# First block's projections by seven block products, with every weight fold ahead of the values

## The chip, the core and the metric

The kernel runs on one core of one Trainium2 chip. TensorE multiplies, ScalarE and VectorE prepare its operands and take results out of PSUM, GpSimd (POOL) issues the transfers that add matrices up in DRAM, and SyncE (SP) issues nearly all other loads. The metric is the device time of one execution in microseconds, lower is better; the time of a kernel is the median of its runs.

## The reference

One decoder layer on a sequence of 2048 tokens of width 1024, and a final norm. This is the part around the change:

```python
h = rmsnorm(x, mix_norm_g[l])
proj = h @ w_in[l]
q, k, v, g, u = jnp.split(proj, [R, 2 * R, 3 * R, 4 * R], axis=-1)
y_ret = jax.nn.silu(g) * head_rmsnorm(retention(q, k, v, positions), ret_gn_g[l])
y_pool = pool_mixer(u, pool_w[l], pool_scale[l])
x = x + jnp.concatenate([y_ret, y_pool], axis=-1) @ w_out[l]
x = x + cross_attn(rmsnorm(x, xa_norm_g[l]), mem_n, xa_wq[l], xa_wkv[l], xa_wo[l])
x = x + conv_glu_ffn(rmsnorm(x, ffn_norm_g[l]), ...)
```

`retention` has four heads of 128 columns with rotary angles on queries and keys, and walks chunks of 128 tokens with a decayed state. `pool_mixer` takes trailing means over 2, 4, 8 and 16 tokens in four groups of 128 columns, subtracts the token and multiplies each group by a 128 x 128 matrix. The cross-attention looks at 256 memory tokens.

## The kernel before, in words

Everything is held transposed: 128 features on the partitions, tokens along the row. The sequence is cut into two blocks of 1024 tokens (`T`), each into two halves of 512 (`SUB`). Every f32 operand is split into a rounded high part and the remainder, by ScalarE and VectorE (`split`, L254), and every product of two such pairs is three matmuls (`passes`, L267; L269 to L271): high by high, high by low, low by high.

**Folds.** Weight matrices that are only ever used one after the other are multiplied ahead of the tokens (`folded_weights`, L423). The memory's keys and values are sixteen projections (`project`, L464), each with eight by three matmuls 256 columns wide. Then for each of four heads the query matrix is folded with the keys into score weights `Md` (L522), and the values with the output matrix into `VWd` (L542); for each of four pooling groups the group's matrix is folded with its rows of the output projection into `WPd` (L566). The results leave by stores that ScalarE issues (`keep`, L487). It is a generator: `folded(n)` (L1998) runs n of its 28 steps. The first sixteen steps, the memory's keys and values, come before block 0's values, with the loads of block 0's x between them (`load_x_wide`, L597; `squares_wide`, L603). The other twelve steps are spread over block 0's heads (`per`, L2033, and `folded(100)`).

**Block 0's projections.** `values` (L732) computes the value columns for all tokens. `head_inputs` (L750) computes gate, query and key columns of one head, each column tile by `unit` (L315): two halves times eight features' tiles times three matmuls, 48 of 512 columns. `pool_group` (L690) does the same for the four pool tiles. The rotary tables are made beside the values (`rope_tables`, L612), after the norm's factors, and scaled by them (`rope_scale`, L671).

**Block 1's projections.** `head_projections` (L1639) takes sixteen column tiles in eight pairs (`PAIRS`, L34) and computes each pair, for the two halves of the 1024 features and the two halves of the tokens, as a two by two block matrix product with seven block products in place of eight (the Winograd form of Strassen's scheme). Each block product is four by three matmuls of 512 columns. What it needs besides: sums of the blocks of x (`quarter_sums`, L1603, on ScalarE and VectorE beside the values), sums of the weights' blocks in DRAM (`Ad`), and additions of results as they leave PSUM (`Heads.evac`). The feed-forward part uses the same scheme for up and down.

**Weight sums.** `weight_sums` (L1012) makes `Ad`, `Ud` (up) and `Dd` (down) by DMAs from DRAM to DRAM that GpSimd issues, four plain and four accumulating ones of 256 KB for each of 8, 22 and 12 jobs. A job takes four turns. A turn comes every `spacing[0]` calls, and each turn waits on a small ScalarE instruction. Before, it starts after the last fold, with spacing 7.

**Order.** The program is written in the order in which steps are yielded, and a scheduling pass then orders each engine's queue; `keep_in_program_order` and `issue_after` pin some instructions. Buffers rotate: five raw buffers of 512 KB for weights (`raws`), three pairs for their split forms (`prs`), ten temporaries (`TT`), five PSUM banks for projections.

Of the kernel before, what the change touches and what calls it, by code (L numbers as in the profile page):

```python
# [136 lines left out]
def trunk(ctx, tc, xT, memT, pos, w_qkgu, w_v, wkv, wqT, wo, wout_r, wout_p, poolT, w_up, w_dn, vecs, consts, outT):  # L137
# [27 lines left out]
    Z = new_z(F32)  # L165
# [257 lines left out]
    def folded_weights():  # L423
# [4 lines left out]
        bank = []  # L428
        raws, first = [Z.take() for _ in range(2)], [new_raw()]
        for q in range(4):  # L430
            to = raws[q // 2].f[:, q % 2 * SUB : (q % 2 + 1) * SUB].rearrange("p (k m) -> p k m", m=NMEM)
            sp.dma_start(to, memT.rearrange("(k p) m -> p k m", p=P)[:, 2 * q : 2 * q + 2])
            if q < 2:
                sp.dma_start(first[0][:, q * SUB : (q + 1) * SUB], wkv[0][:, 4 * q : 4 * q + 4].rearrange("p k n -> p (k n)"))
        first.append(load_tile(wkv[1]))
# [5 lines left out]
        parts = []  # L441
        for k in range(KT):
            h, j = divmod(k, 4)
            split(raws[h].f[:, j * NMEM : (j + 1) * NMEM], mh[:, k], ml[:, k], memg[:, k : k + 1], kept="both")
            if k in (0, 3):
                parts.append(new_pair())
                split(first[0][:, k // 3 * SUB : (k // 3 + 1) * SUB], parts[-1][:, 0], parts[-1][:, 1], kept="both")
        first[0] = parts
        rm = TT.take()
        rn = smp.tile([P, 4], F32, tag="rnm", name="rnm", bufs=1)[:, :2]  # L450

        def memory_norm():
            for r in raws:
                tc.keep_in_program_order(act.activation(r.f, r.f, AF.Square))
            f, other = (r.f for r in raws)
# [4 lines left out]
            for r in raws:  # L460
                r.free()
            spread(rn, [rm.f[:, :NMEM]])

        def project(n):  # L464

            if n < 2:
                hs = first[0] if n == 0 else pairs(first[1])
            else:
                hs = pairs(load_tile(wkv[n]))
# [4 lines left out]
            for k in range(KT):  # L474
                w = [hs[k // 4][:, i, (k % 4) * P : (k % 4 + 1) * P] for i in range(2)]
                passes(ps, w, (mh[:, k], ml[:, k]), k == 0, k == KT - 1)
            return ps

        def row_pairs(src):
            raw = new_raw()  # L480
            sp.dma_start(raw, src)
            u = B.take(2)
            for i in range(2):
                split(raw[:, i * SUB : (i + 1) * SUB], u.r[:, i * SUB : (i + 1) * SUB], u.r[:, T + i * SUB : T + (i + 1) * SUB])
            return u
# [8 lines left out]
        kk = B.take(4)  # L494
        kp4 = kk.r.rearrange("p (n i m) -> p n i m", i=2, m=NMEM)
        ps = [project(n) for n in range(2)]
        sp.dma_start(cs_t, consts)
        memory_norm()
        for n in range(KT):
            if n > 1:  # L500
                ps.append(project(n))
            if n % 2:
                for at in (n - 1, n):
                    t = TT.take()
                    tt(dve, t.f[:, :NMEM], ps.pop(0), rm.f[:, :NMEM], ALU.mult)
                    split(t.f[:, :NMEM], kp4[:, at, 0], kp4[:, at, 1])
                    t.free()
            if n == KT - 1:
                rm.free()
            yield  # L510
        vv = B.take(4)
        vp4 = vv.r.rearrange("p (n i m) -> p n i m", i=2, m=NMEM)
        for n in range(KT):
            ps.append(project(KT + n))
            if n % 2:
                for at in (n - 1, n):
                    split(ps.pop(0), vp4[:, at, 0], vp4[:, at, 1])
            if n == KT - 1:
                mp.free()
            yield  # L520

        for h in range(HEADS):  # L522
            dp = [row_pairs(wqT[(2 * h + dt) * P : (2 * h + dt + 1) * P, :]) for dt in range(2)]
            for k2 in range(KT // 2):
                ps = mmps()
                for j in range(2):
                    for dt in range(2):
                        k = 2 * k2 + j
                        w = [dp[dt].r[:, i * T + k * P : i * T + (k + 1) * P] for i in range(2)]
                        passes(ps[:, j * NMEM : (j + 1) * NMEM], w, (kp4[:, 2 * h + dt, 0], kp4[:, 2 * h + dt, 1]), dt == 0, dt == 1)  # L530
# [5 lines left out]
            for u in dp:  # L536
                u.free()
            if h == HEADS - 1:
                kk.free()
            yield  # L540

        for h in range(HEADS):  # L542
            dp = [row_pairs(wo[(2 * h + dt) * P : (2 * h + dt + 1) * P, :]) for dt in range(2)]
            for mt in range(2):
                for nh in range(2):
                    ps = mmps()
                    for dt in range(2):
                        lh = [vp4[:, 2 * h + dt, i, mt * P : (mt + 1) * P] for i in range(2)]
                        w = [dp[dt].r[:, i * T + nh * SUB : i * T + (nh + 1) * SUB] for i in range(2)]
                        passes(ps, lh, w, dt == 0, dt == 1)  # L550
# [3 lines left out]
            for u in dp:  # L554
                u.free()
            if h == HEADS - 1:
                vv.free()
            yield

        raw = new_raw()  # L560
        r3 = raw[:, :SUB].rearrange("p (g c) -> p g c", g=4)
        sp.dma_start(r3, poolT.rearrange("g p c -> p g c"))
        pw = B.take()
        tt(dve, r3, r3, bcast(pscale, P), ALU.mult)
        split(raw[:, :SUB], pw.r[:, :SUB], pw.r[:, SUB:])
        for g in range(4):  # L566
            u = row_pairs(wout_p[g])
            for nh in range(2):
                ps = mmps()
                lh = [pw.r[:, i * SUB + g * P : i * SUB + (g + 1) * P] for i in range(2)]  # L570
                passes(ps, lh, [u.r[:, i * T + nh * SUB : i * T + (nh + 1) * SUB] for i in range(2)], True, True)
# [3 lines left out]
            u.free()  # L575
            if g == 3:
                pw.free()
            yield
# [18 lines left out]
    def load_x_wide(k, room):  # L597

        f = room[k].f
# [3 lines left out]
    def squares_wide(k, room):  # L603

        f = room[k].f
        tc.keep_in_program_order(act.activation(f, f, AF.Square))
        if k:
            tc.keep_in_program_order(tt(dve, room[0].f, room[0].f, f, ALU.add))
            room[k].free()

# [60 lines left out]
    def rope_scale(tabs, rb):  # L671

        cos, sin = tabs
        out = Z.take(2)
        for s in range(NS):
            ps = slice(64 * s, 64 * s + 64)
            r = rb[s].f[ps, :SUB]
            for hf in range(2):
                po = slice(64 * hf, 64 * hf + 64)
                tt(dve, out.f[po, s * SUB : (s + 1) * SUB], cos.f[ps, :SUB], r, ALU.mult)  # L680
                dve.scalar_tensor_tensor(
                    out=out.f[po, T + s * SUB : T + (s + 1) * SUB],
                    in0=sin.f[ps, :SUB], scalar=1.0 if hf else -1.0, in1=r, op0=ALU.mult, op1=ALU.mult,
                )
        cos.free()
        sin.free()
        return out


    def pool_group(b, g, rb):  # L690
        out = B.take(2)

        def evac(s, ps):
            u, *bufs = [TT.take() for _ in range(3 if g else 2)]
            tt(dve, u.f[:, 16 : 16 + SUB], ps, rb[s].f[:, :SUB], ALU.mult)
            dve.tensor_copy(u.f[:, 0:16], phalo[:, g])
            dve.tensor_copy(phalo[:, g], u.f[:, SUB : SUB + 16])
            src, lo = u, 1
            for i in range(g + 1):
                sh = 1 << i  # L700
                dst = bufs[i % 2]
                tt(dve, dst.f[:, lo : 16 + SUB], src.f[:, lo : 16 + SUB], src.f[:, lo - sh : 16 + SUB - sh], ALU.add)
                src = dst
                lo += 2 * sh
            cur, d = u.f[:, 16 : 16 + SUB], src.f[:, 16 : 16 + SUB]
            w = 2 << g
            if b == 0 and s == 0:
                tt(dve, d[:, :w], d[:, :w], icnt[:, :w], ALU.mult)
                ts(dve, d[:, w:], d[:, w:], 1.0 / w, ALU.mult)
                tt(dve, d, d, cur, ALU.subtract)  # L710
            else:
                stt(d, d, 1.0 / w, cur, ALU.mult, ALU.subtract)
            split(d, out.r[:, s * SUB : (s + 1) * SUB], out.r[:, T + s * SUB : T + (s + 1) * SUB])
            for r in (u, *bufs):
                r.free()

        unit(load_tile(w_qkgu[12 + g]), xpair, evac)
        return out


    def value_weights(kp, room=None):
        raw = new_raw() if room is None else room.f
        sp.dma_start(raw.rearrange("p (k n) -> p k n", k=2), w_v[2 * kp : 2 * kp + 2].rearrange("k p n -> p k n"))
        u = B.take(2)
# [3 lines left out]
        if room is not None:  # L728
            room.free()
        return u  # L730

    def values(rn, wp, step=lambda: None, v=None):  # L732
        v = v or Z.take(4)
# [16 lines left out]
    def head_inputs(h, rb, cs, fill):  # L750
# [1562 lines left out]
```

## Time and profile before

| | |
|---|---|
| median of 3 runs | 2430.71 us (2430.0 to 2430.91) |
| profiled execution, first to last instruction (the page gives it no other time) | 2429.8 us |
| instructions | 33360 |
| moved by DMA | 502.35 MB |

How to read it: an engine's busy time is the time in which it executed something; PE stands for TensorE's matmuls, PEld for its loading of weights, DVE for VectorE, ACT for ScalarE. A row of the table of stretches gives one stretch of the execution. A group of instructions gives its line, engine and operation, its output and inputs, shapes, count, then busy time, mean duration of one, and the engine's idle time just before them with what ended it. A row of the waits gives who waited for whom, the total, the number of times, and the longest. In a row of the timeline stand start and duration in us. A DMA queue's row gives packets, MB and the time of its packets as a share of 16 engines; q1 carries SyncE's transfers, q10 ScalarE's, q0 GpSimd's.

### The profile page before, as it was taken

Reading aid. Unit: us, or ns where it says so; the run is one execution under the profiler, and the core shown is the slowest. Engines: PE = TensorE matmul, PEld = TensorE weight load, DVE = VectorE, ACT = ScalarE, POOL = GpSimd, SP = SyncE. Lnnn points to the kernel's source line nnn. Section 1 sums busy time; section 2 is a strip of 40 time slices with the busy share of each in tenths; the row PEclk is TensorE's granted clock in tenths of the full one; section 3 lists DMA queues with packets and bytes.
Section 4 is the critical chain, followed back from the end, with each engine's and each line's share of the span. In section 5 each row is a group of like instructions: output and inputs, shape, how many; then the busy total and the mean of one; then the engine's idle time right before and its main releaser. Section 6 shows DMA issues by size and latency. Waiting matters only on the chain.

```text
span 2429.8 us, 33360 instructions
## 1 busy us (share of the span) xinstructions
PE 2412.5 (99%) x11328; PEld 2018.4 (83%) x11328; DVE 1722.6 (71%) x2911; ACT 1292.3 (53%) x2360; POOL 306.1 (13%) x477
## 2 busy tenths in 40 slices
PE   9999999999999999999999999999999999999998
PEld 8888888888888888888888888888888888888887
DVE  7756566655857775565788776887677698867875
ACT  6434423444545553334655555765555577666663
POOL 0000012154032444300001010020000000000000
PEclk9999999999999999999999999999999999999999
DMA  7233548699678899985568564755556479758951
GB/s 283 76 105 115 163 137 225 189 237 329 203 206 216 197 254 305 258 293 168 173 223 272 170 204 143 249 191 164 173 158 211 126 244 311 238 183 279 348 178 73
DMA packets 263627, 502.35 MB, mean 207 GB/s; under 512 B 28832, under 2 KB 58016, under 8 KB 263456
## 3 DMA queue, kind: packets, MB, share of 16 engines
q1 hardware_dynamic: 201424, 385.78, 48.3%
q0 software_dynamic: 37376, 86.00, 15.3%
q10 hardware_dynamic: 24656, 28.43, 3.4%
q8 instruction: 89, 1.46, 0.2%
q14 instruction: 82, 0.67, 0.1%
HBM read 398.65 MB, written 187.43 MB: 241 GB/s over the span
## 4 chain that ended last, share of the span: by engine, by line
PE 98%; DVE 1%; ACT 1%; DMA 0%; issue 0%; SPq 0%; DVEq 0%; ACTq 0%
PE mm L269 31%; PE mm L271 30%; PE mm L270 30%; PE aux L269 1%; PE aux L270 1%; PE aux L271 1%; PE aux L832 1%; PE aux L816 1%; PE aux L957 1%; PE aux L805 1%; PE aux L834 1%; DVE Z L241 0%; PE aux L350 0%; PE aux L807 0%; DMA R<-wkv 0%; PE aux L857 0%
## 5 line engine op out<-in xcount | busy, mean ns | idle before, releaser
L269 PE MATMUL mm<-G,Q 128*128 128x512 f32 (+1 forms) x1703 | 656.1, 386 | 3.8 <-ACT Q L257 2.5
L271 PE MATMUL mm<-G,Q 128*128 128x512 f32 (+1 forms) x1703 | 652.9, 384 | 1.4 <-DVE Q L241 1.4
L270 PE MATMUL mm<-G,Q 128*128 128x512 f32 (+1 forms) x1575 | 605.2, 384 | 0.4 <-DVE G L249 0.3
L270 PE MATMUL mm<-G,E 128*128 128x512 f32 x1084 | 421.5, 389 | 0.0
L269 PE MATMUL mm<-G,E 128*128 128x512 f32 x1084 | 420.0, 389 | 0.0
L271 PE MATMUL mm<-G,E 128*128 128x512 f32 x1084 | 419.3, 389 | 0.0
L269 PEld LDWEIGHTS mm<-G,Q 128*128 128x128 f32 x1703 | 320.1, 188 | 67.6 <-ACT Q L257 3.4
L271 PEld LDWEIGHTS mm<-G,Q 128*128 128x128 f32 x1703 | 320.1, 188 | 64.5 <-DVE Q L241 2.0
L270 PEld LDWEIGHTS mm<-G,Q 128*128 128x128 f32 x1575 | 296.0, 188 | 57.3 <-DVE G L249 0.8
L241 DVE TENSOR_TENSOR Z<-Z,mm 128x512 f32<-128x512 f32 (+1 forms) x310 | 207.6, 674 | 121.5 <-PE mm L271 115.7
L249 DVE SCALAR_TENSOR_TENSOR Z<-Z,vecs 128x1024 f32<-128x1024 f32 x176 | 224.8, 1281 | 50.2 <-ACT Z L1191 47.9
L271 PEld LDWEIGHTS mm<-G,E 128*128 128x128 f32 x1084 | 203.5, 188 | 42.4
L270 PEld LDWEIGHTS mm<-G,E 128*128 128x128 f32 x1084 | 203.6, 188 | 42.2
L269 PEld LDWEIGHTS mm<-G,E 128*128 128x128 f32 x1084 | 203.5, 188 | 42.1
L1128 ACT ACTIVATE E<-R 128x512 fp32r<-128x512 f32 (+1 forms) x165 | 101.4, 615 | 144.2 <-PE mm L270 138.3
L241 DVE TENSOR_TENSOR Q<-R,Q 128x512 fp32r<-128x512 f32 x158 | 108.1, 688 | 73.2 <-ACT Q L257 56.0
L241 DVE TENSOR_TENSOR T<-T 128x512 f32<-128x512 f32 (+3 forms) x202 | 138.6, 690 | 21.1 <-ACT T L416 12.1
L241 DVE TENSOR_TENSOR G<-T,G 128x512 fp32r<-128x512 f32 (+1 forms) x185 | 121.6, 677 | 26.5 <-ACT G L1075 13.5
L1075 ACT ACTIVATE G<-T 128x512 fp32r<-128x512 f32 x186 | 112.0, 623 | 32.4 <-DMA T<-Gd 25.7
L1191 ACT ACTIVATE Z<-Z,vecs 128x1024 f32<-128x1024 f32 x88 | 109.1, 1241 | 31.2 <-DVE Z L241 30.2
L1128 ACT ACTIVATE E<-S 128x512 fp32r<-128x512 f32 (+1 forms) x107 | 65.9, 616 | 108.6 <-PE mm L270 106.5
L241 DVE TENSOR_TENSOR E<-R,E 128x512 fp32r<-128x512 f32 (+1 forms) x129 | 86.6, 673 | 44.6 <-ACT E L1128 42.7
(356 smaller groups left out, 3838.2 us busy)
## 6 DMA issues: line engine op xcount, KB each, us to landing
T<-Gd SPq DMA_DIRECT2D x173, 256.0 KB, 4.5
Ud<-w_up POOLq DMA_DIRECT2D x132, 256.0 KB, 9.3
Gd<-Z SPq DMA_DIRECT2D x110, 256.0 KB, 2.8
R<-Ud SPq DMA_DIRECT2D x106, 256.0 KB, 2.7
R<-w_up SPq DMA_DIRECT2D x80, 256.0 KB, 3.1
S<-Ud SPq DMA_DIRECT2D x70, 256.0 KB, 2.8
Gd<-T SPq DMA_DIRECT2D x56, 256.0 KB, 3.4
S<-w_up SPq DMA_DIRECT2D x52, 256.0 KB, 3.2
```

The costliest lines, as they stand in the source:

```text
L241: return eng.tensor_tensor(out=out, in0=a, in1=b, op=op)
L249: return dve.scalar_tensor_tensor(out=out, in0=a, scalar=s, in1=b, op0=op0, op1=op1)
L269: pe.matmul(ps, lh, rh, start=start, stop=False, skip_group_check=more)
L270: pe.matmul(ps, lh, rl, start=False, stop=False, skip_group_check=more)
L271: latest[0] = pe.matmul(ps, ll, rh, start=False, stop=stop, skip_group_check=more)
L805: pe.matmul(col(sc, c), self.ch(k, c), self.ch(q, c), start=True, stop=True)
L816: pe.matmul(col(self.kv, c), col(self.kn.f, c), self.ch(v, c, h * T), start=True, stop=True)
L832: pe.matmul(col(y, c), col(self.pr.f, c), self.ch(v, c, h * T), start=True, stop=self.cur[c] is None)
L834: pe.matmul(col(y, c), self.ch(q, c), self.cur[c], start=False, stop=True)
L1075: one = act.activation(hi, x, AF.Copy, scale=-1.0 if i == 2 else 1.0)
L1128: act.activation(p2[:, 0, :w], self.raw[i].f[:, :w], AF.Copy)
L1191: act.activation(self.c[g].f, a[:, 2:], AF.Identity, bias=cb[:, f : f + 1], scale=cw[2][:, f : f + 1])
```

## The change

1. Block 0 takes the path of block 1 for its query, key, gate and pool columns: `quarter_sums`, `head_projections` and the first three output tiles with weights fetched ahead. `head_inputs`, `pool_group` and `rope_scale` are gone, and `retention` loses its second form.
2. All 28 steps of the folds, and one that frees buffers, run ahead of the values, in a written order in which the memory's projections alternate with the folds that use them. Weights of the folds are split 1024 columns at a time into five wide pairs (four of them in `Z`, one in `Q`) rather than 512 at a time. Keys and values leave PSUM two tiles at a time.
3. x is loaded beside the folds, its squares are added up as each tile arrives, in raw buffers; value weights follow later.
4. Block 0's rotary tables are made at the first keys and stored to DRAM, from where `head_projections` reads them.
5. The weight sums start in the folds' last steps with spacing 2; the eight jobs for these columns start every second turn.

```diff
+        K, V, M, O, W = keys, memory_values, score_weights, output_weights, pool_weights
+        for f, *a in ((K, 0), (K, 1), (K, 2), (K, 3), (K, 4), (K, 5), (M, 0), (K, 6), (K, 7), (M, 1), (V, 0), (V, 1), (M, 2),
+                      (V, 2), (V, 3), (M, 3), (V, 4), (V, 5), (O, 0), (V, 6), (V, 7), (O, 1), (W, 0), (W, 1), (O, 2),
+                      (W, 2), (W, 3), (O, 3), (none_left,)):
+            f(*a)
             yield
...
+        zr = new_z(F32R).t
+        wides = Places([(Q, 0)] + [(zr, 2 * i * T) for i in range(4)], 2 * T)
...
+        def wide_pair(raw, parts=1):
+            u, w = wide(), T // parts
+            for i in range(parts):
+                split(raw[:, i * w : (i + 1) * w], *(r[:, i * w : (i + 1) * w] for r in u))
+            return u
...
         while jobs or live:
-            if jobs:
+            if jobs and (len(jobs) <= others or at % 2 == 0):
                 live.append(jobs.pop(0))
...
+    under[0], spacing[0] = weight_sums(), 2
+    wv, total, tables0 = [], None, stored_tables(0)
+    for n, _ in enumerate(folded_weights()):
+        if n in (1, 2, 3, 4):
+            for _ in range(3):
+                next(tables0, None)
+        if n == 3:
+            total = raws.take()
+        if n in (4, 6, 8, 10, 12, 14, 16, 18):
+            load_x_wide((n - 4) // 2, total)
+        if n == 19:
+            normed = norm_tables([total], late=True)
+        if n in (18, 21):
+            wv.append(value_weights(len(wv), 0))
+        if n in (24, 25):
+            wv.append(value_weights(len(wv), 1))
+        if n > 19:
+            next(under[0], None)
+    Z = new_z(F32)
+    slow[0], paced[0] = False, True
     for b in range(NB):
-        if b == 0:
-            rn, rb, last = normed
-            v = values(lambda: rn, wv)
...
-            per = [(0, 1, 1), (0, 1, 1), (0, 2, 2), (0, 2, 3)]
-            mix = []
-            for h in range(HEADS):
-                qkg = head_inputs(h, rb, cs, lambda i: folded(per[h][i]))
-                mix.append(B.take(2))
-                behind[0] = retention(b, h, qkg, v, mix[h])
-            folded(100)
-            slow[0], paced[0], spacing[0] = False, True, 7
-            pooled = {g: pool_group(b, g, rb) for g in (0, 3, 2, 1)}
...
+        t1, t2 = (B.arenas[0].take(4) for _ in range(2))
+        v, z = Z.take(4), Z.take(4)
+        more_sums = quarter_sums(b, t1, t2, z)
+        next(more_sums)
+        got, place = [], [0]
+        heads = head_projections(b, v, normed[1], t1, t2, z, got)
+
+        def between():
+            next(behind[0], None)
+            if b == 0:
+                next(under[0], None)
```

More of the change, by code (lines that the diff above doesn't have):

```diff
@@ L459, in memory_norm @@
             dve.tensor_copy(rn, stats([f[:, :NMEM]]))
-            for r in raws:
+            for r in memory:
                 r.free()
-            spread(rn, [rm.f[:, :NMEM]])
+            spread(rn, [rm.f[:, :NMEM]], late=True)
         def project(n):
[L466 to L469, printed above, removed]
+            u = u0 if n == 0 else wide_pair(second, 2) if n == 1 else wide_pair(load_tile(wkv[n]))
             if n % 2 == 0:
@@ L690, in pool_group @@
[L690 to L718, printed above, removed]
@@ new lines, in trunk, with weight_half @@
+    Z = new_z(F32)
+    slow[0], paced[0] = False, True
+    for b in range(NB):
+        t1, t2 = (B.arenas[0].take(4) for _ in range(2))
[8 more added lines that the diff above has]
+                next(under[0], None)
+            place[0] += 1
+            for _ in range(2 if place[0] > 2 else 1):
+                next(more_sums, None)
+            if place[0] > 6:
+                if place[0] == 7:
+                    for _ in more_sums:
+                        pass
+                    next(heads)
+                next(heads)
+        values(lambda: normed[0], wv, between, v)
+        finish()
+        rb = normed[1]
+        got.append(v)
+        parts = [next(heads)]
+        mix = got[1]
+        def weight_half():
+            return parts.pop() if parts else next(heads)
```

410 lines of the change are left out of this document (131 added, 279 removed).

## The prediction

> **What bounds the kernel now.** I read the page's head and its chain of waits first, then the table of stretches, then who waits for whom on TensorE, then groups of instructions by shape.
>
> ```profile
> span 2429.8 us, 33360 instructions
> PE 2412.5 (99%) x11328; PEld 2018.4 (83%) x11328; DVE 1722.6 (71%) x2911; ACT 1292.3 (53%) x2360; POOL 306.1 (13%) x477
> PE 98%; DVE 1%; ACT 1%; DMA 0%; issue 0%; SPq 0%; DVEq 0%; ACTq 0%
> ```
>
> TensorE is the chain. A saved matmul is worth its whole step, if nothing else comes last in its place. So I need the step, the places where TensorE does wait, and the load of the other engines wherever the change packs work. In the stretches below, the columns are busy time and count of PE, PEld, DVE, ACT and POOL, then clock, DMA share and GB/s.
>
> ```profile
> 0.00:5.39 5.39, 4.09 (x18) 3.90 (x18) 1.27 (x8) 2.78 (x5) 0.20 (x4) 1.00 0.64 189
> 5.39:42.52 37.13, 35.20 (x272) 33.37 (x272) 32.00 (x67) 27.75 (x48) 0.00 (x0) 1.00 0.89 349
> 42.52:49.40 6.88, 4.74 (x26) 4.54 (x25) 6.88 (x12) 5.72 (x10) 0.00 (x0) 0.75 0.52 175
> 20.00:40.00 20.00, 20.00 (x169) 20.00 (x168) 17.76 (x41) 14.02 (x25) 0.00 (x0) 1.00 0.90 353
> 400.00:420.00 20.00, 20.00 (x90) 16.58 (x89) 9.26 (x15) 6.00 (x11) 1.38 (x3) 1.00 0.91 260
> ```
>
> A 512-wide matmul steps in 20/90 = 0.2222 us, a 256-wide one in 20/169 = 0.1183 us. TensorE loses time only at the start: 272 matmuls need 32.2 us of the second row's 37.13 (4.9 lost), 26 need 3.1 of the third's 6.88 (3.8 lost). In 20 to 40 us it is never idle although VectorE is 89% busy and DMA 90%: close to full, this pipeline still works.
>
> **Part by part. Removed: products.** Block 0's sixteen column tiles took 16 x 2 halves x 8 x 3 = 768 matmuls; eight pairs of seven products take 8 x 7 x 4 x 3 = 672. 96 fewer at 0.2222: **-21.3 us**. Retention and values keep their matmuls.
>
> **Moved: the folds.** Of the scores', output's and pool's folds, 192 matmuls of 256 columns and 120 of 512 leave the head stage, where they cost TensorE their steps and nothing else, and join the 384 of the memory's keys and values. TensorE's part is 576 x 0.1183 + 120 x 0.2222 = 94.8 us; after the 5.4 us before the first fold matmul and the 4.9 us lost early, folds would end at **105.1 us** if TensorE set it. The third row's 3.8 us lies in that stage too; it goes if the new stage is last elsewhere: **-3.8**. The question is what else the stage must do by then. ScalarE's rows:
>
> ```profile
> L606 ACT ACTIVATE Z<-Z 128x1024 f32<-128x1024 f32 x8 | 7.8, 1044 | 0.0
> L260 ACT ACTIVATE G<-Z,vecs 128x1024 fp32r<-128x1024 f32 x8 | 9.1, 1141 | 0.1
> L260 ACT ACTIVATE G<-Z,vecs 128x256 fp32r<-128x256 f32 x8 | 3.6, 499 | 2.1 <-DMA Z<-memT 2.1
> L454 ACT ACTIVATE Z<-Z 128x1024 f32<-128x1024 f32 x2 | 2.0, 1043 | 0.0
> L257 ACT ACTIVATE Q<-R 128x512 fp32r<-128x512 f32 x36 | 22.3, 629 | 48.6 <-PE mm L270 45.7 <-PE aux L374 1.4 <-DMA R<-wkv 0.8
> L534 ACT ACTIVATE T<-mm,vecs 128x256 f32<-128x256 f32 x32 | 13.3, 470 | 6.9 <-PE mm L271 5.2 <-PE aux L857 1.4 <-ACT G L257 0.3
> L552 ACT ACTIVATE T<-mm,rnm 128x512 f32<-128x512 f32 x16 | 11.0, 687 | 7.1 <-PE mm L271 6.9 <-DMA VWd<-T 0.2
> L665 ACT ACT_TABLE_LOAD x1 | 1.3, 1283 | 0.0
> ```
>
> Weights are now split 1024 wide: 16 + 8 + 8 + 4 = 36 splits. No plain one of that width is in the trace; it lies between 7.8/8 = 0.98 and 9.1/8 = 1.14, and I take 1.06: 38.0 us (35 to 41). x: 8 x (1.14 + 0.98) = 16.9. Memory: 3.6 + 2.0. Evacuations: 13.3 + 11.0, and the pool's eight at the 0.62 of L257, 5.0. Splits of 512 (keys, values, value weights, pool): 17 x 0.62 = 10.5. Sines, sign and factor copies with a table load: about 4.5. Sum 104.7 us. And ScalarE issues the 40 stores:
>
> ```profile
> 299.52 0.37 ACTq L488 DMA_DIRECT2D WPd<-T  x1
> 312.62 1.07 ACT L573 ACTIVATE T<-mm 128x512 f32<-128x512 f32 x2
> 313.23 0.93 ACTq L488 DMA_DIRECT2D WPd<-T  x2
> 314.26 1.09 ACT L573 ACTIVATE T<-mm 128x512 f32<-128x512 f32 x2 [0.57 <-ACT T L573]
> 314.88 1.99 ACTq L488 DMA_DIRECT2D WPd<-T  x2
> 317.48 0.60 ACT L573 ACTIVATE T<-mm 128x512 f32<-128x512 f32 x1 [2.14 <-DMA WPd<-T]
> ```
>
> An issue costs 0.37 us, or nothing where it lies beside the instruction before it: 0 to 14.8 us, half taken. In the rows two evacuations with two issues took 1.64 us (312.62 to 314.26) where two alone take 1.07, so half an issue each is shown. ScalarE's first split started at 4.1 us, hence 4.1 + 104.7 + 7.4 = **116 us** (109 to 124). VectorE:
>
> ```profile
> L241 DVE TENSOR_TENSOR Z<-Z 128x1024 f32<-128x1024 f32 x7 | 8.6, 1224 | 1.8 <-ACT Z L454 1.1 <-ACT Z L606 0.3
> L249 DVE SCALAR_TENSOR_TENSOR G<-Z,vecs,G 128x1024 fp32r<-128x1024 f32 x8 | 10.2, 1281 | 0.4 <-issue 0.4
> L249 DVE SCALAR_TENSOR_TENSOR T<-T 128x512 f32<-128x512 f32 x13 | 8.7, 689 | 0.2
> L241 DVE TENSOR_TENSOR T<-T 128x512 f32<-128x512 f32 x4 | 2.8, 692 | 0.1
> L246 DVE TENSOR_SCALAR T<-T 128x512 f32<-128x512 f32 x6 | 2.6, 426 | 0.1
> ```
>
> 36 low parts at 1.23 are 44.3; x 10.2 + 8.6; memory about 6; 21 of 512 at 0.69 (keys, values, value weights, pool) 14.5; the rotary tables, now at the first keys, 13 + 4 + 9 operations, 8.7 + 2.8 + 3.9 = 15.4; norms and factors 7.5. Sum 106.5, from 4.6 us: **111 us**. The tables and the split of x are queued ahead of later low parts on VectorE, and TensorE waits for those.
>
> DMA, in turn the first reads, the two kinds of stores, and the weight sums:
>
> ```profile
> DMA packets 3032, 10.60 MB, mean 408 GB/s; under 512 B 321, under 2 KB 321, under 8 KB 3029
> q10 hardware_dynamic: 4880, 4.46, 12.1%
> q10 hardware_dynamic: 6871, 3.41, 21.4%
> q0 software_dynamic: 2428, 5.35, 62.0%
> q1 hardware_dynamic: 2424, 4.41, 32.1%
> ```
>
> They come from 10 to 36, 130 to 240, 246 to 300 and (the last two) 700 to 740 us. Reads run at 408 GB/s; stores at 4.46 MB / (12.1% of 110 us) = 335 GB/s in long rows and 3.41 / (21.4% of 54) = 295 in short ones; sums at 5.35 / (62% of 40) = 216. The stage reads 27.3 MB (wkv 8.4; x, wq and wo 4.2 each; 6.3 of others): 66.9 us. It stores 10.5 MB of folds and 0.8 of tables: 36.2. Five turns of sums queued on POOL before the values are 19 transfers of 0.262 MB: 23.0. That is 126 us, of which some 17 may land after the last fold: the last stores, eight buffers in flight, the last turn. So **110 us**.
>
> Three resources end at 110 to 116 us where TensorE alone ends at 105.1. Each waits for another, so I add 4 us to the longest (the early 4.9 us of the second row is such a loss): 120, **+14.9** (+4 to +25).
>
> When dense matmuls resume, the clock can be low:
>
> ```profile
> 42.24 0.28 PE L270 MATMUL mm<-G 128*128 128x256 f32 x1
> 44.27 0.39 PE L269 MATMUL mm<-G,Q 128*128 128x256 f32 x1 [1.75 <-ACT Q L257]
> 46.07 0.42 PE L271 MATMUL mm<-G 128*128 128x256 f32 x1
> 46.28 0.41 PE L269 MATMUL mm<-G 128*128 128x256 f32 x1
> ```
>
> After 1.75 us of idleness the steps were 0.21 us instead of 0.12, in a stretch whose granted clock was 0.75: some sixteen steps, 1.5 us. Where TensorE isn't last that is hidden; I count one such spell, ahead of the values: **+1.5** (0 to 3). The Trainium skill, "TensorE: Matmul & The Clock Gate", section "Why this matters for your kernels", asks only for no gaps above about 3 us; by it this term would be nil and the sum 1.5 us lower. The shorter gap here was followed by the lower clock, so the row decides.
>
> **Moved: heads, sums, tables.** Block 0's heads now run as block 1's do, whose whole idleness is
>
> ```profile
> PE aux L805 <- DVE E L249: 1.1, 1, 1.1
> PE mm L269 <- ACT T L1752: 0.8, 1, 0.8
> ```
>
> **+1.9**. Their sums in DRAM must be ready: one job begins every second turn and takes four turns. Five turns come before the values and eight beside them, so the first five pairs' sums are complete when the heads begin and the others by about their tenth product, while a pair's seven products last 7 x 12 x 0.2222 = 18.7 us: none is late. Weights for up and down follow at one turn per two products, denser than in block 1. Mixing, attention and the rest keep their order; nothing counted.
>
> Sum: -21.3 - 3.8 + 14.9 + 1.5 + 1.9 = -6.8 us, span 2423.0. The page gives the profiled execution no time but its span, 0.9 us under the 2430.71 median of the runs: **2424.0 us**. About 0.2% (4.9 us) is what a measurement can tell from no change.
>
> **Rivals.** *Hidden (0.12):* issues cost nothing and values are drawn in among the folds, so that the stage loses 2 us or less beyond TensorE's time: -21.3 - 3.8 + 2 + 1.9 + 0 gives 2409.5; up to 2416. For it: the 20 to 40 us row. Against: four loads at once.
>
> *The last folds starve (0.22), slower:* from the first output fold to the last pool fold TensorE has 96 x 0.2222 + 48 x 0.1183 = 27 us. Its reads are 9.2 MB (22.5 us), its stores 5.25 (17.8), its sums 14 transfers (17.0): 57 us. Eight stores in flight (7.1) and four weight buffers ahead (5.1) leave 45, a stall of 18; with 7 us of ScalarE's and VectorE's before it, 25 in the place of 14.9: 2434.1; without the buffers 2446. The row at 317.48 speaks for it: ScalarE waited 2.14 us for a store there, and TensorE had other work then, which it now hasn't. It decides once the folds end after 105.1 + 21.7 = 126.8 us.
>
> *Sums starve the heads (0.08):* a job is 2.1 MB, 9.7 us at 216 GB/s, and one is due per 5.3 us, beside the products' 0.262 MB per 2.67 us. If those loads fall behind by 0.1 to 0.3 us in each of 56 products, 6 to 17 us are added: 2430 to 2441. Against: with q0 at 62% beside q1, loads were met and TensorE was full. "DMA: Bandwidth & Descriptors" of the Trainium skill, section "Queues, rings and completion order", has each engine take queues in turn by packets; by it the loads keep half, and the rows agree, both queues moving.
>
> *The change doesn't do it (0.02):* were the folds not all ahead, head matmuls would still alternate with them; the time would be near the hidden case.
>
> Likeliest, the sum above (0.50): 2416 to 2429.5; a third of it lies within 0.2%. The rest (0.06) is spread. Faster: 0.35 + 0.12 + 0.06 = 0.53; same 0.19; slower 0.28. The range leaves out the ends of hidden and starved: 2411 to 2439.
>
> **What would show it.** Right: 96 fewer wide products, the folds' last matmul near 120 us, ScalarE over 90% busy until then, TensorE waits there of 10 to 15 us on splits and evacuations. Wrong: TensorE full there (hidden), evacuations waiting for stores with folds past 127 us (starved), or waits on Ad or w_qkgu loads in block 0's heads.

## The result and the profile after

| | before | after |
|---|---|---|
| median | 2430.81 us (4 runs, 2430.0 to 2431.79) | 2485.47 us (4 runs, 2483.35 to 2486.86) |
| ratio, 95% interval | 1 | 1.0226 (1.0211 to 1.024) |
| first store of block 0's residual (`Xd`) | 383.1 us | 437.8 us |
| last store of block 1's residual | 969.4 us | 1023.5 us |

The change is 54.7 us slower. The forecast was 2424.0 (2411 to 2439), a small gain; the kernel lost time, and far outside that range. The last two rows say where to look: 54.7 us are lost by the end of block 0's heads, and nothing is lost or won behind them (969.4 to 1023.5 is 54.1). The page's head, busy times and chain of the profiled execution (its own time 2485.65 us):

```profile
span 2483.9 us, 33353 instructions
PE 2413.6 (97%) x11232; PEld 2013.5 (81%) x11232; DVE 1740.3 (70%) x2869; ACT 1351.4 (54%) x2457; POOL 310.8 (13%) x484
PE 90%; DMA 4%; DVE 3%; ACT 2%; issue 1%; ACTq 0%; SPq 0%; DVEq 0%
```

There are 96 matmuls fewer, exactly as counted, and yet TensorE is busy as long as before: some of the remaining ones ran slowly. And the chain, 98% TensorE before, now has 10% of other things in it. Stretches of after (busy time and count of PE, PEld, DVE, ACT and POOL, then clock, DMA share, GB/s): the first two from the start, up to the first of block 0's eight value results (187.2 us) and to the sixth (215 us; the last is taken out at 224.3), the others inside the folds:

```profile
0.00:187.20 187.20, 133.56 (x770) 119.67 (x771) 102.12 (x152) 102.55 (x153) 10.38 (x22) 0.83 0.76 235
0.00:215.00 215.00, 161.36 (x892) 142.72 (x893) 121.26 (x181) 116.23 (x181) 25.97 (x47) 0.85 0.80 240
20.00:40.00 20.00, 13.41 (x84) 12.71 (x83) 19.25 (x41) 7.44 (x8) 0.00 (x0) 0.80 0.64 212
60.00:80.00 20.00, 12.53 (x87) 12.53 (x88) 11.05 (x11) 12.43 (x19) 0.00 (x0) 0.74 0.56 167
80.00:100.00 20.00, 12.63 (x107) 12.42 (x105) 11.60 (x11) 12.51 (x18) 0.00 (x0) 0.91 0.75 253
```

The last two rows are the ones to learn from: between 60 and 100 us no engine is near full, not even the DMA. Such a stretch isn't bound by any sum of work; something in it waits for something else. (From 20 to 40 us it is otherwise: VectorE is 96% busy.)

The row to 215 us in numbers: the 892 matmuls (578 of 256 columns, 276 of 512, 38 others with 7.4 us) need 578 x 0.1183 + 276 x 0.2222 + 7.4 = 137.1 us at their full step. It is 215 us long: 78 us lost, 53.6 of them idle (215 - 161.4) and 24.3 in matmuls that ran slower than that (161.4 - 137.1; the granted clock of the row is 0.85). The same for before, whose values end at 108 us:

```profile
0.00:108.00 108.00, 102.63 (x624) 92.39 (x625) 79.51 (x156) 63.19 (x104) 0.20 (x4) 0.98 0.54 192
```

386 x 0.1183 + 200 x 0.2222 + 7.4 = 97.5 us of work: 10.5 lost. From 215 us to the end of block 0's output projection (509.8) the new kernel loses another 8 us: 294.8 us for 1103 matmuls of 512 and 312 of 128, which need 286.7, the 312 taken at the 41.6 us that they cost before, where TensorE never stopped behind 108 us. The whole account: -21.3 (the products) - 10.5 + 78 + 8 = +54.2.

What TensorE waited for from 0 to 130 us of after, then what SyncE's queue of loads waited for from 0 to 200 (who waits, for whom, total, times, longest):

```profile
PE mm L268 <- ACT Z L256: 16.0, 3, 11.1
PE mm L268 <- ACT Q L256: 11.0, 2, 10.4
```

```profile
SPq L458 <- DVE Z L240: 26.3, 9, 12.1
SPq L339 <- DVE Z L240: 23.1, 8, 7.0
SPq L614 <- DVE S L240: 9.7, 4, 4.3
```

TensorE waits for high parts (L256), as forecast; but many of the loads that these need are themselves issued late, because the raw buffer that they go into comes free only with a low part (L240) or with x's running sum (`DVE S`). One round of this ring, from the chain of waits of after (start, duration, what):

```profile
54.26 4.03 DMA R<-wqT
58.38 1.07 ACT Z L256
59.47 1.23 DVE Z L240
60.69 1.15 DVE S L240
61.85 4.48 DMA R<-wqT
66.36 1.06 ACT Q L256
67.47 0.58 PE mm L268
68.05 0.22 PE mm L269
68.27 0.21 PE mm L268
```

A load of 4.0 us, its split, the low part, then x's sum, which frees a buffer, then the next load, and only then TensorE, which starts at 0.21 us a step instead of 0.118. x's tiles now live in this ring; before, they had eight places of their own in `Z`, which the change gave to the wide pairs.

### The profile page after: what moved, and what is told of

It reads as the page before. It is cut to its first block, busy times and chain, and to the rows that moved or that the text cites. A ratio compares the mean times of both kernels' runs of the same rounds, so it can differ in the third digit from the quotient of the medians.

```text
span 2483.9 us, 33353 instructions
## 1 busy us (share of the span) xinstructions
PE 2413.6 (97%) x11232; PEld 2013.5 (81%) x11232; DVE 1740.3 (70%) x2869; ACT 1351.4 (54%) x2457; POOL 310.8 (13%) x484
## 4 chain that ended last, share of the span: by engine, by line
PE 90%; DMA 4%; DVE 3%; ACT 2%; issue 1%; ACTq 0%; SPq 0%; DVEq 0%
PE mm L268 28%; PE mm L269 28%; PE mm L270 28%; DVE Z L240 1%; DMA R<-wqT 1%; PE aux L268 1%; PE aux L270 1%; PE aux L269 1%; PE aux L762 1%; PE aux L747 1%; PE aux L855 1%; PE aux L736 1%; DMA Z<-rope_d 1%; PE aux L764 1%; ACT Z L256 0%
## 5 line engine op out<-in xcount | busy, mean ns | idle before, releaser
L268 PE MATMUL mm<-G,Q 128*128 128x512 f32 (+1 forms) x1574 | 611.7, 389 | 13.8 <-ACT Q L256 11.6
L270 PE MATMUL mm<-G,Q 128*128 128x512 f32 (+1 forms) x1574 | 608.1, 388 | 0.2 <-DVE Q L240 0.2
L269 PE MATMUL mm<-G,Q 128*128 128x512 f32 (+1 forms) x1446 | 562.0, 389 | 0.2 <-DVE G L248 0.2
L269 PE MATMUL mm<-G,E 128*128 128x512 f32 x1052 | 409.1, 389 | 0.0
L268 PE MATMUL mm<-G,E 128*128 128x512 f32 x1052 | 407.4, 389 | 0.0
L270 PE MATMUL mm<-G,E 128*128 128x512 f32 x1052 | 406.9, 389 | 0.0
L268 PEld LDWEIGHTS mm<-G,Q 128*128 128x128 f32 x1574 | 297.5, 189 | 75.6 <-ACT Q L256 12.4
L270 PEld LDWEIGHTS mm<-G,Q 128*128 128x128 f32 x1574 | 296.9, 189 | 59.7 <-DVE Q L240 0.4
L269 PEld LDWEIGHTS mm<-G,Q 128*128 128x128 f32 x1446 | 273.5, 189 | 54.0 <-DVE G L248 0.4
L240 DVE TENSOR_TENSOR Z<-Z,mm 128x512 f32<-128x512 f32 (+1 forms) x322 | 215.7, 674 | 126.2 <-PE mm L270 122.0
L270 PEld LDWEIGHTS mm<-G,E 128*128 128x128 f32 x1052 | 197.5, 188 | 41.2
L269 PEld LDWEIGHTS mm<-G,E 128*128 128x128 f32 x1052 | 197.5, 188 | 41.0
L268 PEld LDWEIGHTS mm<-G,E 128*128 128x128 f32 x1052 | 197.4, 188 | 41.0
L240 DVE TENSOR_TENSOR Q<-R,Q 128x512 fp32r<-128x512 f32 (+1 forms) x158 | 111.2, 705 | 69.1 <-ACT Q L256 42.2
L240 DVE TENSOR_TENSOR T<-T 128x512 f32<-128x512 f32 (+4 forms) x196 | 134.4, 690 | 20.9 <-ACT T L415 10.5
L240 DVE TENSOR_TENSOR G<-T,G 128x512 fp32r<-128x512 f32 x165 | 110.2, 688 | 30.3 <-ACT G L975 15.7
L1028 ACT ACTIVATE E<-S 128x512 fp32r<-128x512 f32 (+1 forms) x107 | 65.9, 616 | 106.6 <-PE mm L269 105.1
L240 DVE TENSOR_TENSOR E<-R,E 128x512 fp32r<-128x512 f32 (+1 forms) x125 | 83.7, 672 | 41.8 <-ACT E L1028 38.6
```

The costliest lines, as they stand in the source:

```text
L240: return eng.tensor_tensor(out=out, in0=a, in1=b, op=op)
L268: pe.matmul(ps, lh, rh, start=start, stop=False, skip_group_check=more)
L269: pe.matmul(ps, lh, rl, start=False, stop=False, skip_group_check=more)
L270: latest[0] = pe.matmul(ps, ll, rh, start=False, stop=stop, skip_group_check=more)
L1028: act.activation(p2[:, 0, :w], self.raw[i].f[:, :w], AF.Copy)
```

## The experiments

The theories, with the letters that some expectations use. **R**, the ring: five raw buffers, shared by weights, memory, x and x's sum, set the pace. **Q**: x's loads, when they wait, block SyncE's queue. **P**: having all folds ahead costs it all by itself, whatever the buffers. **T**: the rotary tables on VectorE hold up what TensorE waits for. **W**: the weight sums hold up the folds' stores. **L**: the engines' own work, as the prediction summed it, is the cause. **S**: the sums' transfers cost the heads their 8 us. All times stand beside 2430.6 to 2431.8 of the kernel before on the same chips. One run each, where no interval is given; four runs of one kernel lay up to 3.5 us apart in after and up to 5.1 in e12, so a smaller difference between single runs says little.

**1. Four more buffers in the ring** (e1), in the space that later holds value weights:

```
+    extra = new_e(F32).t
+    for j in range(4):
+        raws.freed.append(len(raws.one))
+        raws.one.append(Arena(extra, j * T, 1, T))
```

> The changed kernel with four more raw buffers of 512 KB (in the part of SBUF that stands empty until the value weights need it), so nine in place of five while the folds run. Theory R (a ring of too few buffers: every load waits for the VectorE part of the split two or more loads before it, and a buffer goes round once per 7 to 9 us): the folds get 45 to 70 us shorter, 2415 to 2440 us. Rival L (the engines' own work in the folds, as the prediction summed it, only packed badly): no change, 2480 to 2490 us. Rival Q (x's loads block SyncE's queue): 5 to 15 us shorter, since x still stands in the same queue.

Measured 2465.04: 20.4 us came back. R is right in kind and too big in size. A stretch of this kernel shows that the folds can run full, with ScalarE, VectorE and DMA all at 74% or more:

```profile
60.00:80.00 20.00, 20.00 (x171) 20.00 (x170) 14.89 (x14) 18.25 (x31) 0.00 (x0) 1.00 0.93 315
```

**2. x's loads issued by GpSimd** (e2):

```
-        tc.keep_in_program_order(sp.dma_start(f, xT[k * P : (k + 1) * P, :T]))
+        tc.keep_in_program_order(pool.dma_start(f, xT[k * P : (k + 1) * P, :T]))
```

> The changed kernel with x's eight loads issued by GpSimd, whose queue is empty then, in place of SyncE; the same five raw buffers. Rival Q (a load of x that waits for its buffer holds up the weights behind it on SyncE): 20 to 40 us shorter, 2445 to 2465 us. Theory R: the number of buffers and the round trip stay, at most 10 us shorter, 2475 to 2487 us. Rival L: no change.

Measured 2485.51, no change. Q falls: it doesn't matter who issues x's loads.

**3. The kernel before with all folds ahead** (e3): its own eight products, buffers and places for x.

```
+    folded(4)
...
+    folded(100)
```

> The kernel before, with eight products and its own buffers (x in eight places of its own, five raw buffers for weights alone, splits 512 wide), but with all twelve later folds run ahead of the values. Theory R: the move itself costs little, because x takes no raw buffer: 10 to 25 us over the 2430.8 of before, 2441 to 2456 us. Rival P (the move costs what it costs in the changed kernel, whatever the buffers): 67 us or so over before, 2490 to 2505 us. Rival L: 15 us over before.

Measured 2448.34, +16.5. P as the whole cause falls, but the move has its price. Two stretches of this run:

```profile
60.00:80.00 20.00, 20.00 (x169) 20.00 (x168) 10.97 (x18) 16.75 (x39) 0.00 (x0) 1.00 0.89 291
80.00:100.00 20.00, 16.46 (x77) 12.98 (x76) 9.10 (x14) 14.23 (x28) 0.00 (x0) 0.91 1.03 353
```

TensorE is full from 60 to 80 us; in the output folds, from 80 us on, the DMA is at its limit and TensorE waits. The +16.5 is close to the +14.9 of my sum of work, but my sum ended with ScalarE at 116 us and had the DMA done at 110, so that the two agree so closely is in part luck.

**4. Sums every sixth turn from block 0's values on** (e4), `spacing[0] = 6` in place of 2.

> The changed kernel with the weight sums at one turn per six products once the values are done, in place of one per two. Rival S (the sums, at a DMA share over 1.0 in the heads, are what the heads of block 0 lose): the heads' 8 us come back, 2475 to 2479 us. Theory R has nothing to say of the heads; if the one long wait there (3.3 us at 421 us, and the low clock after it) comes from the chain of a head and not from DMA: 2483 to 2487 us.

Measured 2482.89, 2.6 less, which isn't clear of noise. From the first value result to the first store of `Xd` the heads take 250.6 us in after and 247.9 here, but also 248.7 in e2 and 247.5 in e5, where the heads are as in after. So S isn't shown, and most of the heads' 8 us stays open.

**5 and 6. The tables later**, in the change (e5) and with nine buffers (e6):

```
-        if n in (1, 2, 3, 4):
+        if n in (10, 11, 13, 14):
```

> The changed kernel, five raw buffers, with block 0's rotary tables made at the fold steps 10, 11, 13 and 14 in place of 1 to 4. Theory T (the tables stand in front of the memory norm's chain on VectorE, so that the first keys cannot leave PSUM): 8 to 20 us shorter, 2465 to 2477 us. Theory R alone (the ring of five raw buffers sets the pace throughout): no change within 4 us. Rival L (VectorE's sum is what counts, and the tables are as long there as here): no change.

> Nine raw buffers and the tables at steps 10 to 14. If R and T both hold, the two gains add or more: 20 to 35 us below the 2465.0 of nine buffers alone, 2430 to 2445 us. If the tables' place is nothing: 2463 to 2467 us.

Measured 2485.99, no change, and 2469.29, 4.2 more than e1 (one run each). At this point T seemed to fall; runs 12 and 13 show that this was too quick.

**7 and 8. No sums before the values**, with nine buffers and later tables (e7), and in the change alone (e8):

```
-        if n > 19:
-            next(under[0], None)
```

> As the one before it, and the weight sums begin with the values in place of nine steps before the end of the folds. Theory W (ScalarE's stores stand behind the sums on the DMA engines: one store's issue took 6 to 7 us, ScalarE is blocked, the pool folds' results stay in PSUM and TensorE's clock falls): 8 to 15 us less than the one before, 2420 to 2435 us. If the stores are slow by themselves: within 3 us of the one before. If the eight column sums then come too late for the heads, slower, with waits on loads of Ad.

> The changed kernel, five raw buffers, tables where they were, with only the weight sums moved to the values. Theory W: 8 to 15 us shorter, 2470 to 2478 us. If the ring of raw buffers hides what the sums cost: 0 to 4 us shorter.

Measured 2463.36, 5.9 less than e6, and 2477.66, 7.8 less than after. ScalarE's timeline at the end of after's folds shows the mechanism (start, duration; ACTq is ScalarE's queue, issuing):

```profile
160.44 0.40 ACTq L519 DMA_DIRECT2D WPd<-T  x1
168.41 6.91 ACTq L519 DMA_DIRECT2D WPd<-T  x2
175.42 0.60 ACT L577 ACTIVATE T<-mm 128x512 f32<-128x512 f32 x1 [7.57 <-issue]
```

An issue of 0.40 us became 6.91 for two, and the evacuation behind them on the same engine stood for 7.57 us. The stretch of these microseconds has every engine nearly idle and the DMA full:

```profile
168.00:176.00 8.00, 1.31 (x6) 0.75 (x4) 0.33 (x1) 0.58 (x1) 0.48 (x1) 0.71 1.05 282
```

GpSimd had just issued six transfers of sums (164.5 to 168.5). In e8, without them, the same place looks like this, and TensorE is busy throughout from 160 us on:

```profile
164.36 0.60 ACT L577 ACTIVATE T<-mm 128x512 f32<-128x512 f32 x1 [0.90 <-DMA WPd<-T]
164.39 3.79 ACTq L519 DMA_DIRECT2D WPd<-T  x4
160.00:170.00 10.00, 10.00 (x45) 8.03 (x44) 1.80 (x2) 5.33 (x9) 0.00 (x0) 1.00 1.09 356
```

Four issues took 3.79 us and the evacuation before them waited 0.90, at a DMA share as high as in after. So W is right, and it is the sums in the queues that matter, not the full DMA alone.

**9. Nine buffers, tables early, no sums before the values** (e9), e1 and e8 together.

> Nine buffers (which gave back 20.4 us alone) and the weight sums only from the values on (7.8 alone), the tables at their place as in the change. If the ring and the stores behind the sums are two separate prices, the gains add: 2485.5 - 28.2 = 2457. If the sums cost time only because the ring was short (the store that waits holds a buffer of the ring), the two overlap: 2461 to 2465. If more sums in the folds had filled time that stands idle anyway, taking them out brings nothing here: 2465.

Measured 2453.93: 31.5 less than after, 3.3 more than the two gains together (28.2), which is within the spread of single runs. They are separate prices.

**10. Four buffers for x alone, five for the rest** (e10), with e8's edit:

```
+    own_x = Places([(extra, j * T) for j in range(4)], T)
...
-            total = raws.take()
+            total = own_x.take()
...
-        r = total if k == 0 else raws.take()
+        r = total if k == 0 else own_x.take()
```

> The eight tiles of x and their running sum get four buffers of their own, the weights keep the five of the change; weight sums from the values on. The ring theory as I now hold it: a buffer is held about 8.5 us for a tile of weights and 11 for one of x, so the change asks 41 x 8.5 + 8 x 11 + about 110 for the running sum + 60 for the memory = 610 buffer-us of five buffers, 122 us at the least; without x it asks 410 of five, 82 us, less than the 105 us of TensorE's own work. So x was what overfilled the ring, and this comes within 4 us of the kernel with nine buffers for all, 2453 to 2461. If it was the number of weight tiles in flight that mattered, it gains only half of the 20: 2466 to 2472. If the ring had nothing to do with x: 2476 to 2479, the gain of the sums alone.

Measured 2451.73, 25.9 less than e8 and level with nine buffers for all. There are nine buffers in both, so the gain is again that of four more; but with x and its running sum in them, the five that are left serve weights and memory as well as nine shared ones do. In that sense it was x with its running sum that overfilled the ring.

**11. Four buffers in place of five** (e11), `raws.freed.remove(4)` until the values begin.

> The change with four buffers in place of five until the values begin; nothing else moved. The ring theory: 610 buffer-us of four are 152 us at the least in place of 122, so the folds end some 30 to 45 us later: 2515 to 2530. If the folds are held by a chain of single steps (load, split, product, store) whatever the count of buffers, five were enough for it and four cost little: 2486 to 2496.

Measured 2501.92, +16.4: more than a chain of single steps would lose, about half of what the ring alone would. So my 610 buffer-us divided by the number of buffers is no law. With four, five and nine buffers the first value result is taken out at 204.4, 187.2 and 162.8 us; what else makes up a round, the runs don't show.

**12. The tables last** (e12), e10 with steps (20, 22, 25, 27) for the tables.

> The kernel with x apart and the sums later (2451.73), with the angle tables made in steps 20, 22, 25 and 27, behind the last tile of x, in place of steps 1 to 4. There the profile has TensorE idle or slow from 20 to 60 us (26.6 of 40 us busy): VectorE takes the memory norm's small steps from 25.4 to 43.7 us between low parts of 1.2 us and steps of the tables of 0.7, and the first keys wait for that norm. If the tables hold up the norm, as I now think, the 12 steps or so between (about 8 us) go from this chain and come back where VectorE is idle: 2442 to 2447. If the norm waits for the low parts and for loads instead, as the run with later tables and five buffers said: 2450 to 2454. If the tables' stores at the end get into the way of the last folds: above 2455.

Measured 2470.79 (2466.84 to 2471.94; ratio 1.016, 1.0143 to 1.0177), 19 us worse than e10. Both halves of this are in its stretches. e10 first, then e12:

```profile
20.00:40.00 20.00, 11.78 (x81) 11.07 (x79) 17.41 (x36) 6.32 (x6) 0.00 (x0) 0.83 0.81 308
40.00:60.00 20.00, 14.77 (x99) 14.19 (x100) 12.72 (x20) 14.52 (x24) 0.00 (x0) 0.74 0.53 163
```

```profile
20.00:40.00 20.00, 15.37 (x108) 14.83 (x108) 13.43 (x28) 10.88 (x17) 0.00 (x0) 0.83 0.78 299
40.00:60.00 20.00, 20.00 (x170) 20.00 (x169) 17.19 (x16) 19.14 (x28) 0.00 (x0) 1.00 0.85 292
100.00:120.00 20.00, 3.23 (x5) 1.40 (x6) 19.04 (x44) 7.48 (x12) 0.00 (x0) 0.55 0.49 158
```

From 20 to 60 us the tables had indeed been in the way: 278 matmuls in place of 180. e10's VectorE there (timeline) does the memory norm's steps of 0.15 us one at a time between steps of the tables:

```profile
37.49 0.15 DVE L248 SCALAR_TENSOR_TENSOR sm<-sm,sm 128x2 f32<-128x2 f32 x1
37.61 0.69 DVE L240 TENSOR_TENSOR T<-T 128x512 f32<-128x512 f32 x1
38.22 0.15 DVE L240 TENSOR_TENSOR sm<-sm 128x2 f32<-128x2 f32 x1
38.34 0.43 DVE L245 TENSOR_SCALAR T<-T 128x512 f32<-128x512 f32 x1
```

But at the end the same work came ahead of x's norm, and in place of one wait there was a larger one. Waits of e12, TensorE's and SyncE's:

```profile
PE aux L373 <- DVE Q L240: 22.2, 3, 17.3
```

```profile
SPq L686 <- ACT T L674: 10.1, 1, 10.1
```

The second row is the other trap: the tables' stores stand in the queue of loads and wait there for ScalarE's sines. e7 has the same row with 3.9 us ahead of a load of x, and the chain to TensorE's longest wait there (15.1 us, until 113 us) runs through it: x's load, its split and sum, then a load for an output fold. In e6 it is alike (15.8 us). That is the likely reason why later tables brought e6 nothing; e1 has the row too, with 8.3 us, but at 33 to 41 us, while TensorE waited for the memory's norm anyway.

**13. The tables one step at a time between the two norms** (e13), their stores off SyncE's queue:

```
-        if n in (1, 2, 3, 4):
-            for _ in range(3):
-                next(tables0, None)
+        if 5 < n < 18:
+            next(tables0, None)
...
-            sp.dma_start(rope_d[i], r.f[:, :SUB])
+            (sp if b else pool).dma_start(rope_d[i], r.f[:, :SUB])
```

> The kernel with x apart and the sums later (2451.73), the tables' twelve steps made one each in steps 6 to 17, between the memory's norm and x's, and their three stores issued by GpSimd, so that SP's queue of loads isn't stopped. If tables ahead of a norm are the open cost: the gain of the last run from 20 to 60 us (8.8 us of TensorE) without its loss of 17.3 us, 2440 to 2445. If the tables' work on VectorE costs as much wherever it stands (low parts and x late instead of the norm): 2449 to 2454.

Measured 2444.09 (2441.82 to 2445.39; ratio 1.0053, 1.0036 to 1.007): as expected, 7.6 less than e10. The edit moves the tables and their stores at once, and no run tells the two apart. What is left (stretches and TensorE's waits up to 180 us):

```profile
40.00:60.00 20.00, 20.00 (x171) 20.00 (x170) 19.21 (x25) 16.86 (x27) 0.00 (x0) 1.00 0.67 208
80.00:100.00 20.00, 17.42 (x101) 14.89 (x99) 18.69 (x22) 19.94 (x28) 1.83 (x3) 1.00 1.01 343
100.00:120.00 20.00, 12.61 (x39) 9.42 (x40) 13.11 (x28) 8.92 (x14) 0.00 (x0) 0.57 0.69 234
```

```profile
PE aux L373 <- DVE Q L240: 6.7, 2, 6.5
PE aux L349 <- DVE E L240: 3.2, 1, 3.2
```

From 80 to 100 us the DMA is full (1.01), as in e3; TensorE waits for x's norm (the two waits, which end at 100.6 and 110.5 us), in a stretch whose clock is 0.57.

**14. The same with sparser sums** (e14), spacing 6. In this kernel the heads read some sums in DRAM before they are made (block 0's last load of one is issued at 333.8 us, the last addition to them at 365.9), so its time leaves out the wait for them.

> The same, with one quarter sum on GpSimd every sixth turn in place of every second during the first block's values and heads. Alone in the change this gave back 2.6 us. If the heads' loss comes from the sums' transfers: 2 to 4 us under the run beside it. But here the sums begin only with the values, so the later readers may now wait for sums that aren't there: then 5 us or more above the run beside it.

Measured 2440.89 (2439.01 to 2443.55; ratio 1.0044, 1.0029 to 1.0059). No more can be said than that even without that wait it isn't as fast as the kernel before.

One view ties the runs together, the start of the sixteen instructions that take out the values (line, name, count, shortest, median and longest duration in ns, first and last start); after, then e13:

```profile
L710 ACT ACTIVATE Z<-mm,rn x16: 667/689/692, 187.2 to 741.5; 128x512 f32<-128x512 f32 x16
```

```profile
L710 ACT ACTIVATE Z<-mm,rn x16: 669/687/690, 144.2 to 699.2; 128x512 f32<-128x512 f32 x16
```

| against after | first value result | time |
|---|---|---|
| four buffers (e11) | +17.2 | +16.4 |
| sums later (e8) | -8.3 | -7.8 |
| nine buffers (e1) | -24.4 | -20.4 |
| x apart, sums later (e10) | -33.7 | -33.7 |
| and tables between the norms (e13) | -43.0 | -41.4 |

A microsecond at the end of the folds is about one of the kernel. (e6, e7 and e12 don't follow this line so closely: their first value result is 13.5, 24.3 and 27.3 us earlier, their time 16.2, 22.1 and 14.7 less; later waits, such as e12's, took some of it back or gave more.)

## Why the prediction was wrong, point by point

- **Products, -21.3:** right; 11232 matmuls in place of 11328.
- **Before's early stall, -3.8:** it went, but into a stage with far larger ones, so it was no gain.
- **The folds, +14.9 (+4 to +25): this step failed.** It read "Three resources end at 110 to 116 us where TensorE alone ends at 105.1. Each waits for another, so I add 4 us to the longest". The sums of work were about right: the split that I took at 1.06 us was 1.06, the low part 1.22 for 1.23, and up to 187.2 us ScalarE was busy for 102.6 us and VectorE for 102.1, where I had 104.7 and 106.5 (the DMA's share there, 0.76, makes 142 us where I had 126). But ScalarE, which was to be over 90% busy, was busy for 55% of this time: the last pool weights were evacuated at 175.4 us and the last output weights at 184.8, where I had the last matmul of the folds near 120. In a loop of buffers the end isn't the largest sum plus a little. It hangs on how long each holder keeps a buffer and on the order of each queue: 2501.9, 2485.5 and 2465.0 us with four, five and nine buffers and the same work. The 20 to 40 us row of before, by which I held that "close to full, this pipeline still works", belonged to a pipeline with x outside the ring and no tables in it. I counted the change's new tenants as work on engines, and didn't ask where they would stand: x and its sum in the ring (25.9 us, e10 against e8), the tables ahead of the norms, with their stores (7.6, e13 against e10), and the sums ahead of the stores (7.8, e8).
- **The move by itself:** +16.5 in e3, close to the 14.9. As an estimate of the work the sum was fair, though its nearness here is in part luck (e3); as an estimate of the change, it lacked the buffers.
- **One spell of low clock, +1.5 (0 to 3):** 24.3 us lost in slow matmuls in the first 215 us. Idle stretches come with low clocks behind them, so a price per stall must include the matmuls that follow. The row that the term rests on was also read too simply: the steps behind the 1.75 us gap in before were at first mostly at 0.12 us, and went to 0.21 at 45.9 us, behind a second gap of 0.39.
- **Heads like block 1's, +1.9:** 8 us. In part it is one wait, for rows that ScalarE scales: `PE aux L777 <- ACT T L772`, 3.3 us in after; the rest is open.
- **Rivals.** "The last folds starve" named a real mechanism, stores behind sums, worth 7.8 us (e8) where I priced a stall of 18 for reads, stores and sums together, and its sign, folds past 126.8 us, came. But when the first output fold began, at 117.9 us, some 50 of the 78 us were lost already (an estimate: 528 matmuls of 256, 62.5 us at their full step, and 5 us of small ones were done). It also counted "four weight buffers ahead" as a head start, when the buffers are a rate. "Sums starve the heads" (6 to 17 us) wasn't seen: TensorE's waits from 187 to 445 us of after, 4.6 us in all, end with ScalarE or VectorE, none with a load. "Hidden" fell with the first trace. No rival held the time: all took the pipeline before as given.

Of the 76 us by which the change misses its saving (2485.5 against 2430.8 - 21.3 = 2409.5), the runs place 41.4 one after the other: 7.8 sums, 25.9 x in the ring, 7.6 tables. The two steps between rest on single runs, so each share may be off by some 3 us; the 41.4 rests on four runs on either side. Of the 34.6 that e13 still lacks, e3's 16.5 and the heads' 8 would be the most, if they carry over, which isn't shown; some 10 us have no place. x's norm, with 9.7 us of TensorE's waits in e13, is the likeliest, and wasn't tried. No kernel here beats the one before: what the seven products save, the folds' move and the heads take back.

## What to carry to other kernels

Before work is moved into a stage, list for every buffer who holds it, for how long, and who comes in new; if holders' time divided by buffers comes near the stage's length (here some 122 us by the estimate ahead of e10, for a stage forecast to end at 120), the sums of the engines don't give its end. Ask the same of each in-order queue: a chain of small steps that TensorE waits for (a norm) must have nothing long queued between its steps, and a store that waits must not stand in the queue that issues loads. When a stretch has no engine near full, as from 60 to 100 us here, look for one of these two.

## What the runs showed of the hardware

- A stall costs more than its gap: behind a wait of 10.4 us in after, the first 23 matmuls, 256 wide, took 5.0 us (67.5 to 72.5 us), 0.22 each, and the ones behind them 0.118. The granted clock from 60 to 80 us was 0.74. That agrees with the Trainium skill, "TensorE: Matmul & The Clock Gate", section "Why this matters for your kernels", which warns of gaps above about 3 us; the gaps of 1.75 and 0.39 us in before, behind which the clock fell too (0.52 from 46.5 to 49.4 us), stay outside its rule.
- An issue of a store on ScalarE took 0.40 us, and 6.91 for two while the DMA share was 1.05 (168 to 176 us) with sums in GpSimd's queue; the evacuation behind it on ScalarE waited 7.57 us. Without the sums, at a share of 1.09, four took 3.79 us (e8).
- A 512 KB load landed in 4.2 to 5.5 us up to 187 us of after (medians of the loads of wkv, wqT, wo and x), four to five times the 1.06 us of the split that follows it. A round is thus mostly load, and more loads in flight helped: four more buffers gave 20.4 us (e1).
